# GDN and mLSTM layers on one core: order of the first products, and the first head's second gate in seven products

## The chip, the cores and the metric

The kernel runs on one core of a Trainium2 chip. The time is the device time of one execution in microseconds. The core's engines are TensorE (PE, matmuls), VectorE (DVE), ScalarE (ACT), GpSimd (POOL) and SyncE (SP, whose queue issues the transfers). TensorE's clock has two levels, 1.2 and 2.4 GHz; the profile gives the granted clock as a share of the full one.

## The reference

x has 1024 tokens of 1024 channels. Two residual layers follow each other, a gated DeltaNet (GDN) and an mLSTM, and then a final RMSNorm. Each has 8 heads, with 128 channels for queries and keys and 256 for values.

```python
def gdn_mixer(h, w_in, ...):                    # layer 0, h = rmsnorm(x)
    qkv, z, a, bt = split(h @ w_in)
    q, k, v = split(silu(causal_dwconv(qkv)))   # q and k are then l2-normed
    g, beta = -exp(a_log) * softplus(a + dt_bias), sigmoid(bt)
    o = gated_delta_chunked(q, k, v, g, beta)
    return (rmsnorm(o) * silu(z)) @ w_out

def mlstm_mixer(h, w_in, ...):                  # layer 1, h = rmsnorm(x + y0)
    qk, v, og, z, ig, fg = split(h @ w_in)
    q, k = split(silu(causal_dwconv(qk)))
    hc = mlstm_chunked(q, k * 128 ** -0.5, v, ig + i_bias, log_sigmoid(fg + f_bias))
    gate = sigmoid(og) * silu(z)                # the first gate and the second gate
    return (rmsnorm(hc) * gate) @ w_out
```

## The kernel before, in words

**Layout.** Everything is kept with channels on the 128 partitions. h is eight tiles of channels (k), each in two halves of 512 tokens. Every operand of a large product is split into a big part (`hi`, rounded, made by ScalarE) and a small part (`lo`, the rest, made by VectorE or GpSimd), and a product is the sum of three matmuls: hi x hi, hi x lo, lo x hi. For h these parts are `hh` and `hl` (lines 261 to 270, `prenorm`: eight products on VectorE, eight casts on ScalarE, eight subtractions; `VLO` names those that VectorE does).

**Projections.** A plain projection (`proj_half`, line 290) takes 128 columns of a weight and one half of the tokens: 8 tiles k of three matmuls with 512 columns each. A `Pair` (line 563) takes 256 columns and both halves together in seven products in place of eight: each product is four tiles of three matmuls, on blocks of h (A11, A12, A21, A22) and on sums of these blocks (S1, S2, S3 from `h_blocks`, line 469, S4 from `last_block`, line 484). It needs sums of weight blocks as well, which VectorE makes (`operands`), and additions on the way out.

**Order.** PE's instructions are issued in the order in which the program writes them. On the other engines a planner orders by readiness in its own simulation and by program order; `tc.issue_after` holds instructions behind a given one. Generators yield after each step (on PE mostly three matmuls), and tables say at which step of the projections a piece of other work is written: `FIRST` for the first mLSTM head, `KEYS`, `QUERIES`, `MERGE`, `TOKENS`, `SCAN`, `BLOCKS`, `LAST` for the GDN heads (first, second, others), `NORM0` for the norm of the second half of h.

**The GDN start.** `first_qk` runs, for each half of the tokens, k's projection and then q's. In the first half each tile of k is followed by two matmuls of the gate columns (`gate_columns`). The norm of the second half is written between steps: its sums (`n_cs`) and the reciprocal root at step 4, the broadcast (`n_rs`) and the parts of h at step 9. In the second half the gate columns run first, then k, then q.

**The first mLSTM head.** After its keys, queries and half of its values the loop at line 1559 runs 80 steps: 16 of values for the second half of the tokens (`mlstm_v`), then 64 of `first_gates`, which computes the output gate (`mog`) and the second gate (`mz`) by plain projections, two column tiles of two halves of eight steps each. In `FIRST` the letters stand for: `g` the gate rows (`head_gates`: a chain of small operations), `p` the decay masks and the scaled keys (`mlstm_prepare`, which first makes `mkd` and later `mg`), `b` one tile of `h_blocks`, `l` one tile of `last_block`, `r` the first weights of the next pair, `s` the first steps of the scan. After the loop the pairs of the other heads follow, while the scan of this head goes on.

## Time and profile before

| | |
|---|---|
| three timed runs | 1934.71, 1935.31, 1938.71 us; median 1935.31 |
| profiled execution | 1938.76 us, its span 1937.0 us |
| PE busy | 1876.3 us (97%), 9776 matmuls |
| VectorE, ScalarE, GpSimd busy | 1252.5, 1010.6, 697.9 us |
| mean granted clock | 0.994 |

A busy PE is not one at its peak: matmuls are pipelined, and their starts, not their lengths, give the pace. Times in the rows count from the start of the span. An idle stretch matters where it is PE's, since PE is busy nearly all the time.

### The profile page before, as it was taken

The numbers are of one execution on the slowest core, as the hardware profiler recorded it, in microseconds if no ns is written. First come the engines' busy times: TensorE is split into PE (matmuls) and PEld (weight loads), VectorE is DVE, ScalarE is ACT, GpSimd is POOL, SyncE is SP. The second block draws the span as 40 slices with busy tenths as digits, with TensorE's granted clock in tenths as the row PEclk, the third lists the DMA queues.
The fourth block names the chain that finished last, engine by engine and source line by source line (L and its number), as shares of the span: only waits on it lengthen the run. The fifth ranks groups of instructions, "written<-read, shape, count | busy, mean of one in ns | idle before, by whom it ended". The sixth has DMA issues, their size and how long they took to land.

```text
span 1937.0 us, 28865 instructions
## 1 busy us (share of the span) xinstructions
PE 1876.3 (97%) x9776; PEld 1548.2 (80%) x9776; DVE 1252.5 (65%) x2845; ACT 1010.6 (52%) x2332; POOL 697.9 (36%) x661
## 2 busy tenths in 40 slices
PE   5899999999999999999999999999999999999998
PEld 3687888887787778787878788888888888888886
DVE  6679686858585858647556866666666666673413
ACT  5555455555555565645445454555554545564423
POOL 4234334343434333100121334333333333345553
PEclk9999999999999999999999999999999999999999
DMA  4211122222222222646321221212122212245342
GB/s 143 79 60 44 55 72 82 56 81 63 69 67 73 71 62 76 205 135 217 116 77 57 79 74 60 76 56 80 63 76 69 74 62 73 76 138 172 137 138 73
DMA packets 138620, 171.24 MB, mean 88 GB/s; under 512 B 30860, under 2 KB 68584, under 8 KB 138472
## 3 DMA queue, kind: packets, MB, share of 16 engines
q1 hardware_dynamic: 137896, 168.87, 27.7%
q8 instruction: 77, 1.26, 0.3%
q14 instruction: 71, 0.58, 0.1%
q10 hardware_dynamic: 576, 0.52, 0.1%
HBM read 142.87 MB, written 26.48 MB: 87 GB/s over the span
## 4 chain that ended last, share of the span: by engine, by line
PE 81%; DVE 6%; ACT 5%; DMA 3%; issue 1%; POOL 1%; SPq 0%; DVEq 0%; ACTq 0%; POOLq 0%
PE lout L699 8%; PE gzp_ps L500 7%; PE gout L699 7%; PE mkq_ps L500 7%; PE mv_ps L500 7%; PE gkv_ps L500 7%; PE mz_ps L500 6%; PE mog_ps L500 6%; PE gqv_ps L500 6%; PE o L1066 1%; PE mo L1487 1%; PE y L1049 1%; PE mv_ps L1237 1%; PE ks L1044 1%; PE sn L1056 1%
## 5 line engine op out<-in xcount | busy, mean ns | idle before, releaser
L414 POOL TENSOR_TENSOR g_r<-g_r,mhalf 128x1 f32<-128x1 f32 x64 | 39.9, 623 | 209.3 <-DVE g_r L413 207.5
L284 DVE SCALAR_TENSOR_TENSOR gw_lo<-gw_raw,rest,gw_hi 128x256 fp32r<-128x256 f32 x128 | 64.4, 540 | 64.3 <-ACT gw_hi L283 64.3
L279 POOL TENSOR_TENSOR lw_lo<-lw_raw,lw_hi 128x512 fp32r<-128x512 f32 x56 | 72.7, 1301 | 72.6 <-ACT lw_hi L278 67.0
L279 POOL TENSOR_TENSOR mog_lo<-mog_raw,mog_hi 128x512 fp32r<-128x512 f32 x39 | 50.3, 1291 | 115.1 <-ACT mog_hi L278 115.1
L283 ACT ACTIVATE gw_hi<-gw_raw,rest 128x256 fp32r<-128x256 f32 x128 | 57.9, 501 | 62.5 <-PE gout L699 36.2
L699 PE MATMUL lout<-lgp_hh,lw_hi 128*128 128x512 f32 x224 | 88.4, 395 | 1.2 <-DVE mg L1357 1.2
L279 POOL TENSOR_TENSOR mz_lo<-mz_raw,mz_hi 128x512 fp32r<-128x512 f32 x39 | 53.1, 1363 | 99.7 <-ACT mz_hi L278 99.7
L699 PE MATMUL lout<-lgp_hh,lw_lo 128*128 128x512 f32 x224 | 87.3, 390 | 0.0
L699 PE MATMUL lout<-lgp_hl,lw_hi 128*128 128x512 f32 x224 | 87.2, 389 | 0.0
L279 POOL TENSOR_TENSOR mv_lo<-mv_raw,mv_hi 128x512 fp32r<-128x512 f32 x38 | 52.4, 1379 | 84.9 <-ACT mv_hi L278 55.2
L500 PE MATMUL gkv_ps<-hh,gkv_hi 128*128 128x512 f32 x176 | 78.2, 444 | 0.0
L278 ACT CAST lw_hi<-lw_raw 128x512 fp32r<-128x512 f32 x56 | 34.7, 620 | 79.1 <-PE lout L699 52.2
L279 POOL TENSOR_TENSOR gkv_lo<-gkv_raw,gkv_hi 128x512 fp32r<-128x512 f32 x40 | 52.2, 1304 | 63.2 <-ACT gkv_hi L278 58.4
L279 POOL TENSOR_TENSOR mkq_lo<-mkq_raw,mkq_hi 128x512 fp32r<-128x512 f32 x35 | 45.1, 1289 | 76.0 <-ACT mkq_hi L278 66.7
L279 POOL TENSOR_TENSOR gzp_lo<-gzp_raw,gzp_hi 128x512 fp32r<-128x512 f32 x38 | 50.4, 1325 | 56.7 <-ACT gzp_hi L278 46.0
L500 PE MATMUL gkv_ps<-hh,gkv_lo 128*128 128x512 f32 x176 | 69.3, 394 | 0.0
L500 PE MATMUL gkv_ps<-hl,gkv_hi 128*128 128x512 f32 x176 | 69.1, 393 | 0.0
L279 POOL TENSOR_TENSOR gqv_lo<-gqv_raw,gqv_hi 128x512 fp32r<-128x512 f32 x30 | 38.8, 1292 | 81.6 <-ACT gqv_hi L278 41.4
L699 PE MATMUL gout<-glp_hh,gw_hi 128*128 128x512 f32 x160 | 66.5, 415 | 0.0
L414 POOL TENSOR_TENSOR m_r<-m_r,mhalf 128x1 f32<-128x1 f32 x64 | 42.8, 669 | 64.1 <-DVE m_r L413 58.9
L699 PE MATMUL gout<-glp_hh,gw_lo 128*128 128x512 f32 x160 | 62.7, 392 | 0.0
L699 PE MATMUL gout<-glp_hl,gw_hi 128*128 128x512 f32 x160 | 62.4, 390 | 0.0
(773 smaller groups left out, 6657.9 us busy)
## 6 DMA issues: line engine op xcount, KB each, us to landing
gw_raw<-in_gdn_w_out_dram SPq DMA_DIRECT2D x64, 256.0 KB, 2.7
lw_raw<-in_mlstm_w_out_dram SPq DMA_DIRECT2D x56, 256.0 KB, 2.7
gzp_raw<-in_gdn_w_in_dram SPq DMA_DIRECT2D x32, 256.0 KB, 3.3
growb<-g_dram SPq DMA_DIRECT2D x32, 256.0 KB, 3.2
gg_dram<-gv_h SPq DMA_DIRECT2D x64, 128.0 KB, 1.8
gl<-gg_dram SPq DMA_DIRECT2D x32, 256.0 KB, 3.2
mog_raw<-in_mlstm_w_in_dram SPq DMA_DIRECT2D x32, 256.0 KB, 3.2
mz_raw<-in_mlstm_w_in_dram SPq DMA_DIRECT2D x32, 256.0 KB, 3.0
```

Source lines behind the costliest of these rows:

```text
L278: A.copy(hi, raw)
L279: (e or G).tensor_tensor(lo, raw, hi.bitcast(F32), ALU.subtract)
L283: A.activation(hi[:, k], raw[:, k], AF.Copy, scale=c)
L284: V.scalar_tensor_tensor(lo[:, k], raw[:, k], c, hi.bitcast(F32)[:, k], ALU.mult, ALU.subtract)
L414: G.tensor_tensor(r, r, mhalf[:, :1], ALU.pow)
L500: mm(ps, w_[:, k, :], h_, start=first and k == 0 and i == 0, stop=k == 3 and i == 2, skip_group_check=True)
L699: mm(pss[2 * j + i], a[:, e, i * P:(i + 1) * P], b, start=h == heads[0] and e == 0 and m == 0, stop=h == heads[-1] and e == ET - 1 and m == 2)
L1044: mm(ks[:, :DV], k[:, s_], S, start=True, stop=True)
L1049: mm(yp[:, :DV], st["tt"][half][:, cc, :], rr, start=True, stop=True)
L1056: mm(spn[:, :DV], st["kd"][half][:, cc, :], w, start=True, stop=True)
L1066: mm(op[:, :DV], st["at"][half][:, cc, :], w, start=S is None, stop=True)
L1237: mm(ps[c], h_[k][half][:, c * P:(c + 1) * P], w_[:, k % 2, :], start=k == 0 and i == 0, stop=k == KT - 1 and i == 2)
```

## The change

Three things change.

In the GDN start, k's projection of head 0 and the gate columns use the small part of tile n four tiles behind the big part (`LAG`, `behind_by`): steps 0 to 3 have big parts only, steps 4 to 6 use the small parts 0 to 2, and step 7 the small parts 3 to 7. The matmuls are the same. The norm of the second half moves to steps 8 and 10.

In the GDN plan, the steps of the head-0 queries, the second head's merge and scan, the last token step of the other heads, the first block of `h_blocks` and the four of `last_block` move.

In the mLSTM layer, the first head's second gate (z) becomes a `Pair`. The loop has 76 steps: 16 of values, 32 of the output gate, 28 of the pair. For this one pair (`late`) the second product is A12 in place of S2, and its weights are split in that order. `h_blocks` moves from steps 42, 46, 50, 54 to 16, 22, 27, 32 and is no longer held behind the gate rows; `last_block` from 72 to 78 to 41 to 47; the two `mg` steps from 54 and 60 to 51 and 56; the pair's weights are loaded at step 26, and two of its operands are split at steps 39 and 42 (`a`). The silu of z is written in place for every head.

```diff
@@ -32,9 +32,11 @@
 NB = P // BLK
 NG4 = P // (NB * NT)
 HT = 4
-NORM0 = (4, 9)
+NORM0 = (8, 10)
 NORM1 = ((-1, 4, 8), (-1, 9, 15))
 RAW = 3
+
+LAG = 4
 QB, AB = 4, 4
 WB, GB = 2, 2
 OUT0 = "k", "wraw"
@@ -44,8 +46,8 @@
 R8 = range(8)
 LOOK = 2
 VLO = (((1, 3, 6, 7), (1, 2, 3, 5, 7)), ((3, 6, 7), (1, 3, 5, 7)))
-FIRST = {0: "g", 13: "g", 18: "g", 23: "g", 28: "g", 33: "p", 37: "p", 42: "b", 46: "b", 50: "b", 54: "bp", 60: "pr", 68: "s",
-         72: "l", 74: "l", 76: "l", 78: "l"}
+FIRST = {0: "g", 13: "g", 16: "b", 18: "g", 22: "b", 23: "g", 26: "r", 27: "b", 28: "g", 32: "b", 33: "p", 36: "p", 39: "a", 41: "l",
+         42: "a", 43: "l", 45: "l", 47: "l", 51: "p", 56: "p", 67: "s"}
 UNITS = ({u: "ss" for u in range(14, 27, 2)},
          {0: "v", 1: "v", 2: "vt", 3: "vp", 4: "p", 6: "p", 8: "p", 11: "s",
           **{u: "ss" for u in (13, 15, 17, 19, 22, 24, 26)}, 28: "s"})
@@ -54,15 +56,15 @@
 
 
 KEYS = ((4, 9, 10, 17), (26, 29, 30, 33), (22, 25, 26, 29))
-QUERIES = ((19, 22, 25, 32), (68, 71, 76, 76), (80, 80, 84, 89))
+QUERIES = ((20, 22, 25, 32), (68, 71, 76, 76), (80, 80, 84, 89))
 SOLVE = (24, 41, 38)
-MERGE = (78, 96, 89)
-TOKENS = ((37, 37, 81, 85), (74, 77, 100, 106), (64, 74, 103, 106))
-SCAN = (95, 113, 102)
+MERGE = (78, 97, 89)
+TOKENS = ((37, 37, 81, 85), (74, 77, 100, 106), (64, 74, 103, 109))
+SCAN = (95, 110, 102)
 PACE = ((3, 3, 8), (4, 3, 10), (4, 3, 11))
-BLOCKS = (101, 115, 114, 126)
+BLOCKS = (106, 115, 114, 126)
 XLOADS = (24, 116)
-LAST = (156, 158, 157, 159)
+LAST = (158, 148, 156, 164)
 TH = HT * P
 
 
@@ -287,12 +289,21 @@
     def split_halves(w, c0, name, raws=None):
         return [split(t, f"{name}_{i}") for i, t in enumerate(raws or load_halves(w, c0, name))]
 
-    def proj_half(parts, name, half, sink):
+    def behind_by(k, lag):
+
+        return range(max(k - lag, 0), KT) if k == KT - 1 else range(k - lag, k - lag + 1) if k >= lag else ()
+
+    def proj_half(parts, name, half, sink, lag=0):
         ps = pwork(f"{name}_ps{half}", "p")
         for k in range(KT):
             hi, lo = parts[k // 4]
-            for i, (w_, h_) in enumerate(((hi, h_hi), (hi, h_lo), (lo, h_hi))):
-                mm(ps, w_[:, k % 4, :], h_[k][half], start=k == 0 and i == 0, stop=k == KT - 1 and i == 2)
+            mm(ps, hi[:, k % 4, :], h_hi[k][half], start=k == 0, stop=False)
+            if lag:
+                mm(ps, lo[:, k % 4, :], h_hi[k][half], start=False, stop=False)
+            for n in behind_by(k, lag):
+                mm(ps, parts[n // 4][0][:, n % 4, :], h_lo[n][half], start=False, stop=lag > 0 and n == KT - 1)
+            if not lag:
+                mm(ps, lo[:, k % 4, :], h_hi[k][half], start=False, stop=k == KT - 1)
             if k == KT - 1:
                 sink(half, ps)
             yield
@@ -349,7 +360,7 @@
                 for _ in gates:
                     pass
             for parts, nm, sink in ((kparts, "k", sinks[0]), (qparts, "q", sinks[1])):
-                for _ in proj_half(parts, f"{name}{nm}0", half, sink):
+                for _ in proj_half(parts, f"{name}{nm}0", half, sink, LAG if name == "g" and nm == "k" else 0):
                     if step < KT:
                         next(gates)
                     between(step)
@@ -565,6 +576,7 @@
 
 
         spare = False
+        late = False
 
         def __init__(self, w, ca, cb, name, sink, dst=lambda e, half: None, u2=None, engines=None,
                      in_psum=(True, True), bank="x"):
@@ -583,8 +595,11 @@
             yield part(1, b11, G)
             V.tensor_tensor(b12, b12, b22, ALU.subtract)
             V.tensor_tensor(b11, b11, b12, ALU.subtract)
-            yield part(6, b11, e6)
+            if not self.late:
+                yield part(6, b11, e6)
             yield part(2, b21, G)
+            if self.late:
+                yield part(6, b11, e6)
             V.tensor_tensor(b21, b21, b11, ALU.subtract)
             V.tensor_tensor(b11, b22, b11, ALU.subtract)
             yield part(5, b11, e5)
@@ -601,13 +616,15 @@
             yield from product(p1, "A11", operand())
             A.copy(u2, p1)
             yield
-            p6 = pwork(f"{name}_ps6", "b")
-            yield from product(p6, "S2", operand())
-            V.tensor_tensor(u2, u2, p6, ALU.add)
-            yield
-            yield from product(p1, "A12", operand(), False)
-            sink(0, 0, p1)
-            yield
+            for second in (self.late, not self.late):
+                if second:
+                    yield from product(p1, "A12", operand(), False)
+                    sink(0, 0, p1)
+                else:
+                    p6 = pwork(f"{name}_ps6", "b")
+                    yield from product(p6, "S2", operand())
+                    V.tensor_tensor(u2, u2, p6, ALU.add)
+                yield
             u4 = wp.tile([P, TH], F32, tag="wraw", bufs=WB, name=f"{name}_u4")
             p5 = pwork(f"{name}_ps5", "p")
             yield from product(p5, "S1", operand())
@@ -741,7 +758,7 @@
     accs = [squares_of(half * HT, HT, f"n0_{half}", "at", AB) for half in range(2)]
     prenorm(0, 0, rstd_of(sums_of(accs[0], "n0_0"), "n0_0"))
 
-    def gate_columns(raw, name, res):
+    def gate_columns(raw, name, res, lag=0):
 
         n = 2 * H
 
@@ -752,9 +769,9 @@
         for half in range(2):
             ps = pwork(f"{name}_ps{half}", "d")
             for k in range(KT):
-                for i, h_ in enumerate((h_hi, h_lo)):
-                    mm(ps[:2 * n, :], wg[:, k, :], h_[k][half], start=k == 0 and i == 0,
-                       stop=k == KT - 1 and i == 1)
+                mm(ps[:2 * n, :], wg[:, k, :], h_hi[k][half], start=k == 0, stop=False)
+                for m in behind_by(k, lag):
+                    mm(ps[:2 * n, :], wg[:, m, :], h_lo[m][half], start=False, stop=m == KT - 1)
                 if k == KT - 1:
                     row = hp.tile([2 * n, TH], F32, tag="acc", bufs=3, name=f"{name}_row{half}")
                     A.copy(row, ps[:2 * n, :])
@@ -775,7 +792,7 @@
     gt = sp.tile([P, 2 * H, NT], F32, tag="td", bufs=1, name="gt")
 
     def gdn_gates():
-        yield from gate_columns(wg0, "ggate", gt)
+        yield from gate_columns(wg0, "ggate", gt, LAG)
         V.tensor_tensor(hc(a_t), gt[:, :H, :], dtb.unsqueeze(2).to_broadcast([P, H, NT]), ALU.add)
         A.activation(hc(beta), gt[:, H:, :], AF.Exp, scale=-1.0)
         V.tensor_scalar(beta, beta, 1.0, None, ALU.add)
@@ -1349,12 +1366,9 @@
             A.activation(gate(half)[:, e, :], src, AF.Sigmoid)
 
         def z_sink(e, half, src):
-            sz = src
-            if h == 0:
-                sz = hp.tile([P, TH], F32, tag="acc", bufs=3, name=f"msz{h}_{e}_{half}")
-            A.activation(sz, src, AF.Silu)
+            A.activation(src, src, AF.Silu)
             g = gate(half)[:, e, :]
-            V.scalar_tensor_tensor(g, g, mnw[:, e:e + 1], sz, ALU.mult, ALU.mult)
+            V.scalar_tensor_tensor(g, g, mnw[:, e:e + 1], src, ALU.mult, ALU.mult)
 
         return o_sink, z_sink, lambda e, half: gate(half)[:, e, :]
 
@@ -1365,12 +1379,11 @@
 
     def first_gates(st):
 
-        o_sink, z_sink, _ = gate_sinks(0, st)
-        for nm, c0, sink in (("mog", 2 * QK + DI, o_sink), ("mz", 2 * QK + 2 * DI, z_sink)):
-            for e in range(ET):
-                parts = split_halves(w1, c0 + e * P, f"{nm}0_{e}")
-                for half in (1, 0):
-                    yield from proj_half(parts, f"{nm}0_{e}", half, lambda half, ps: sink(e, half, ps))
+        o_sink = gate_sinks(0, st)[0]
+        for e in range(ET):
+            parts = split_halves(w1, 2 * QK + DI + e * P, f"mog0_{e}")
+            for half in (1, 0):
+                yield from proj_half(parts, f"mog0_{e}", half, lambda half, ps: o_sink(e, half, ps))
 
     def parts_of(t, hi, lo, name, e=G):
 
@@ -1548,21 +1561,22 @@
         sts_m = [st] + [{"v": []} for _ in range(H - 1)]
         pairs = []
         for h in range(H):
-            if h:
-                pairs += gate_pairs(h, sts_m[h])
+            pairs += gate_pairs(h, sts_m[h])[0 if h else 1:]
             if h < H - 1:
                 pairs += [keys_pair(h + 1, sts_m[h + 1]), values_pair(h + 1, sts_m[h + 1])]
-        for pair in pairs[1::2]:
+        for pair in pairs[::2]:
             pair.spare = True
+        pairs[0].late = True
         sources.extend(sources_of(pairs))
         todo = iter(pairs)
-        for i, _ in enumerate(steps_of(mlstm_v(0, st, 1, vparts, VT[1]), first_gates(st))):
+        for i, _ in enumerate(steps_of(mlstm_v(0, st, 1, vparts, VT[1]), first_gates(st), next(todo).products())):
             for g in FIRST.get(i, ""):
                 if g == "b":
-                    with tc.issue_after(st["gates"].ins):
-                        do(hb)
+                    do(hb)
                 elif g == "r":
                     pairs[0].load()
+                elif g == "a":
+                    ahead(len(ready) + 1)
                 else:
                     do({"g": hg, "p": prep, "l": lb, "s": scan}[g])
         ahead(LOOK)
```

## Rows read from the trace of the kernel before

**Rows 1.** The page, sections 1 and 4: busy share of engines; chain by engine.

```profile
PE 1876.3 (97%) x9776; PEld 1548.2 (80%) x9776; DVE 1252.5 (65%) x2845; ACT 1010.6 (52%) x2332; POOL 697.9 (36%) x661
...
PE 81%; DVE 6%; ACT 5%; DMA 3%; issue 1%; POOL 1%; SPq 0%; DVEq 0%; ACTq 0%; POOLq 0%
```

**Rows 2.** PE's waits: waiter, line, released by; us in total, times, longest.

```profile
PE gk_ps L295 <- DVE hl L270: 4.0, 1, 4.0
...
PE mg L1414 <- DVE mkd_lo L1405: 2.5, 1, 2.5
...
PE ggate_ps L756 <- DVE hl L270: 1.9, 1, 1.9
...
PE kq L940 <- DVE nt L914: 1.0, 1, 1.0
```

**Rows 3.** PE's timeline, head: start, length, line, operation, [idle before, releaser].

```profile
21.52 0.80 PE L295 MATMUL gk_ps<-hh,gk_hi 128*128 128x512 f32 x1 [2.44 <-ACT hh L269]
...
29.35 0.79 PE L295 MATMUL gk_ps<-hl,gk_hi 128*128 128x512 f32 x1 [4.04 <-DVE hl L270]
...
36.59 0.95 PE L235 MATMUL n_cs<-ones,n_sq 128*128 128x1 f32 x8
...
40.96 0.39 PE L295 MATMUL gq_ps<-hh,gq_hi 128*128 128x512 f32 x1
...
42.36 1.02 PE L258 MATMUL n_rs<-n_diag,ones 128*128 128x512 f32 x2
...
55.15 0.50 PE L295 MATMUL gk_ps<-hh,gk_hi 128*128 128x512 f32 x1
```

**Rows 4.** Stretches: us; busy of PE, PEld, DVE, ACT, POOL; PE clock; DMA.

```profile
28.50:35.30 6.80, 5.95 (x14) 3.73 (x15) 3.80 (x6) 0.00 (x0) 0.24 (x1) 0.50 0.00 0
1026.00:1048.00 22.00, 22.00 (x146) 19.32 (x144) 6.80 (x25) 9.36 (x16) 1.56 (x2) 1.00 0.12 39
1048.00:1072.00 24.00, 21.52 (x98) 17.31 (x97) 22.62 (x39) 18.47 (x38) 6.60 (x4) 0.95 0.30 98
```

**Rows 5.** VectorE's timeline, head of the program.

```profile
27.75 2.75 DVE L270 TENSOR_TENSOR hl<-x,hh 128x512 fp32r<-128x512 f32 x3
...
31.02 0.68 DVE L270 TENSOR_TENSOR hl<-x,hh 128x512 fp32r<-128x512 f32 x1
...
38.87 0.69 DVE L251 TENSOR_TENSOR n_diag<-ident,n_rc 128x512 f32<-128x512 f32 x1 [1.12 <-POOL n_rc L249]
...
43.42 4.04 DVE L266 SCALAR_TENSOR_TENSOR x<-x,nwc,n_rs 128x512 f32<-128x512 f32 x6
```

**Rows 6.** ScalarE's timeline, head of the program.

```profile
23.15 3.52 ACT L269 CAST hh<-x 128x512 fp32r<-128x512 f32 x6
...
48.87 1.28 ACT L318 ACT_TABLE_LOAD   x1
```

**Rows 7.** PE's timeline, first mLSTM head.

```profile
1062.32 0.50 PE L295 MATMUL mz_ps<-hh,mz_hi 128*128 128x512 f32 x1
...
1069.92 2.08 PE L1414 MATMUL mg<-mqT,mkT 128*128 128x128 f32 x8 [2.46 <-DVE mkd_lo L1405]
...
1076.49 1.05 PE L1414 MATMUL mg<-mqT,mkT 128*128 128x128 f32 x8
...
1091.05 0.39 PE L500 MATMUL mkq_ps<-hh,mkq_hi 128*128 128x512 f32 x1
```

**Rows 8.** The chain that ended last, second gate: start, us, what.

```profile
1083.72 7.49 PE mz_ps L295 x33
```

**Rows 9.** VectorE's timeline, and tile S4hl: ns min/median/max, first and last start.

```profile
1066.01 1.79 DVE L458 TENSOR_TENSOR S3hl<-hs,S3hh 128x512 fp32r<-128x512 f32 x1
...
1069.53 0.59 DVE L1405 SCALAR_TENSOR_TENSOR mkd_lo<-mtp,wkey,mkd 128x128 fp32r<-128x128 f32 x2
...
L458 DVE TENSOR_TENSOR S4hl<-hc,S4hh x4: 673/686/693, 1082.5 to 1097.6; 128x512 fp32r<-128x512 f32 x4
```

**Rows 10.** GpSimd's timeline, same stretch.

```profile
1063.37 3.88 POOL L279 TENSOR_TENSOR mz_lo<-mz_raw,mz_hi 128x512 fp32r<-128x512 f32 x2 [10.25 <-ACT mz_hi L278]
```

## The prediction

> **What bounds the kernel now.** I read the page first. TensorE (PE) is busy for 97% of the span and holds 81% of the chain that ended last [rows 1]. A change can therefore pay in three ways only: fewer matmuls, fewer idle gaps on PE, or less time at the lower clock. The second view was the list of PE's waits [rows 2]. Besides the start of the program it is short, and four of its stalls stand where the change works: 4.0 us for a small part of h, 1.9 us for another in the gate columns, 1.0 us ahead of the first kq, and 2.5 us ahead of mg in the first mLSTM head. The third view was PE's timeline of the head of the program [rows 3] with the granted clock by stretch [rows 4]: after the 4.0 us stall PE ran 28.5 to 35.3 at 0.50 (1.2 of 2.4 GHz), where a 512-column matmul takes 0.43 us (14 in 5.95) instead of 0.23 [rows 8]. Then I read the engines that feed these places [rows 5, 6], and the same for the first mLSTM head [rows 7 to 10].
>
> **GDN: small parts four tiles behind.** No matmul is added or removed; the order alone changes. PE begins gk at 21.52 [rows 3]. The big parts hh come from ScalarE, six of them in 3.52 us from 23.15, the last at about 26.7 [rows 6]; three of the four small parts that VectorE makes come at 27.75 to 30.5 [rows 5]. In the old order the second k tile needs its small part, and PE stops from 25.3 to 29.35. In the new order steps 0 to 3 need only big parts. Walked through (three matmuls in steps 0 to 3, five in 4 to 6, thirteen in 7, 40 in all): steps 0 to 2 are paced by the low clock and the arrival of hh until about 25.4; from there a matmul takes 0.23 if the clock then rises as it did in the profiled run and does not fall. Step 3 ends at 26.1 and step 4 at 27.2. Step 5 waits for the first VectorE small part until about 28.7 (a third of the way through the group at 27.75) and ends at 29.4. Step 6 ends at 30.5 and step 7, held a little by the last small part near 31.7 [rows 5], at 33.5. The old end of the same work was 40.96 with the n_cs sums inside it (0.8), so 40.15. That is 6.6 us.
>
> Not all of it is kept, because the sums of the second half are now queued behind this work (step 8 instead of 4) and the norm at step 10 instead of 9. In the old run n_cs started at 36.59 and the diagonal was ready at 39.56 [rows 3, 5], 2.97 us later, with slack before n_rs at 42.36. New: n_cs starts at 34.2, the diagonal is ready at 37.2, and only six matmuls (1.4 us) stand between n_cs and n_rs: PE waits about 0.8 us, a new wait, with the rest of gq half 0 queued behind it. n_rs then starts at 37.2 to 38, 4.4 to 5.1 us earlier than before. From n_rs to gk half 1 the old run took 12.8 us (42.36 to 55.15), paced by eight products on VectorE from 43.42, the casts on ScalarE, the subtractions, and the gate columns behind them. Here a little more goes: a table load of 1.28 us for the first silu on ScalarE [rows 6] stood among the casts, and part of the convolution of gk among the products; both now come due before them. I take 1 us for that. So gk half 1 starts 5.5 us earlier. From below: if the norm of the second half is the whole limit and the queues shift against it, 2 us; from above, if nothing is lost, 7.5 us. The kq step (20 instead of 19) gives three more matmuls (0.7 us) of cover to a 1.0 us stall [rows 2]: 0.7 us, between 0 and 1. The other moved steps (merge, scan and tokens of later heads, the blocks, the last block) carry the same instructions at other places in PE's order. They add and remove no work on PE; I cost them at nothing, since VectorE's fillers are hidden behind 97% of matmul, with plus or minus 3 us as the bound: 3 us is about what one stall like mg's with its clock is worth (below). The scan of head 1 now begins one step after its last merge product, so a ScalarE copy has 0.7 us instead of 3.4 us to land; that is inside the 3.
>
> **mLSTM: the first head's second gate in seven products.** Old: four half projections of 24 matmuls, 96. New: seven products of 12, 84. In the chain 33 such matmuls took 7.49 us [rows 8], 0.227 each: 12 x 0.227 = 2.7 us less on PE. This is as good as certain.
>
> The old stage ran from 1062.32 to 1091.05 [rows 7], 28.7 us. Of that 96 x 0.227 = 21.8 is mz; 2.5 is the wait for mg; two groups of mg at full clock are 2.1 (the second one's 1.05 each); six scan matmuls of half the columns are some 0.7 (an estimate, half of 0.227 each); the rest, 1.7 us, is the clock: the first mg group took 2.08 instead of 1.05 and the matmuls behind it ran slow, right after the wait. So that wait is worth 2.5 + 1.7 = 4.2 us.
>
> Does it go? mg waits for a PSUM buffer that mkd_lo reads; the last of its readers ends at 1069.9 [rows 9]. These run in turns with ScalarE's mkd copies and were late because VectorE was full: 22.62 us of 24 in 1048 to 1072, after only 6.80 of 22 in 1026 to 1048 [rows 4]. What filled it were the block sums, held back behind the gates. The change moves the four h_blocks steps to 16, 22, 27, 32 and drops that hold. Each is six 128x512 operations on VectorE of 0.68 us (the S4 row's median [rows 9]), 4.1 us, 16.3 us for four, and the idle 15.2 us of 1026 to 1048 is where they can now go. Against it: mg stands at step 51 instead of 54, 2 us earlier; the last block (four times four operations, 10.9 us) is now due at steps 41 to 47; and the pair brings eleven VectorE operations that the plain projection did not have (four differences of weights, two small parts, five additions), 7.5 us, four more ScalarE casts and copies, and one more GpSimd subtraction. The pair's four weight loads are as large as the four that they replace; they are issued at step 26, past nothing that waits. The loads of mkq's weights now follow at step 39, ahead of the decay rows for mg on SyncE's queue, and the first of them waits for a buffer that the pair frees; if SyncE holds to that order, the rows come late for the second chunk of the scan, which has some 15 steps to spare. The silu of z in place costs what it did: the same four activations and products. I cost the loads and the silu at nothing, and their bound is the stage's. Work on VectorE from 1026 to PE's need of S4 near 1079 is then about 6.8 + 16.3 + 10.9 + 7.5 + 7 (the attention's own masks, mkd_lo and products) = 48.5 us in 53. It fits, barely, so I don't expect PE to pass without any wait: I put 2 us back. Net: 2.7 + 4.2 - 2 = 4.9 us; from below 0 (waits of 7 us), from above 7.
>
> At one place a page speaks against this. The row: with GpSimd in two mz_lo subtractions (3.88 us [rows 10]) a VectorE subtraction took 1.79 us instead of 0.68 [rows 9]. The Trainium skill, "SBUF — State Buffer", section "Who interferes with whom", says that a VectorE instruction with two SBUF inputs and a GpSimd instruction that reads SBUF exclude each other on a shared port. The trace agrees. By that rule each of the pair's five GpSimd subtractions would cost VectorE up to 1.1 us, 5.5 us in all, and the sum of the stage would be nearer its lower end.
>
> **Sum.** 5.5 + 0.7 + 4.9 = 11.1 us. Against the profiled execution: 1938.8 - 11.1 = 1927.7. The three timed runs have their median 3.4 us below that execution (1935.3, one of the three as high as it); the same difference gives 1935.3 - 11.1 = 1924.2.
>
> **The rivals.** *VectorE takes it back in the mLSTM stage.* Lockstep chain, S sums and S4 on one full engine; mg at step 51 waits as long as before, and the clock falls again. For it: 22.62 of 24 us, the exclusion above, mg earlier by three steps. Against it: 15 idle us ahead of it. The stage nets 0: 1935.3 - 5.5 - 0.7 = 1929.1.
>
> *The second half's norm takes back the head.* PE gets to n_rs early and waits there, and again in the gate columns, since that chain hangs on VectorE and ScalarE. For it: the 1.9 us stall there now. Against it: sums and diagonal are earlier too. The head nets 1: 1935.3 - 1 - 0.7 - 4.9 = 1928.7.
>
> *Slower: S4 comes too late.* In the old run the four small parts of S4 ended between 1083 and 1098.3 [rows 9], and nobody wanted them before the sixth product of mkq, 20 steps of 0.68 us after 1091.05 [rows 7]. Now the sixth product of mz wants the last near 1080.5 (1062.3 + 23 steps of 0.68 + mg and scan). If VectorE's fillers don't move forward, PE waits 17.8 us and loses about 2 at the low clock, as after mg: 1935.3 + 19.8 - 2.7 - 4.2 - 6.2 = 1942.0. It decides the sign once the last part is later than about 1091. The single buffer hc, in which each block waits for the one before, speaks for it; the free stretch before speaks against it.
>
> *Both gains lost.* First and second rival together leave about 1 us: 1934.5, no change that can be told.
>
> **How the numbers follow.** Forecast 0.50, first rival 0.21, second 0.13, slower 0.08, no change 0.08. The predicted time is the forecast's, 1924.2, its own range 1919 to 1929. For 8 in 10 the range takes in the first two rivals and the 3 us of the moved steps on either side: 1917 to 1932. About 0.2%, 3.9 us, is what a measurement of this kernel can tell from no change: faster by more 0.83, within it 0.08, slower by more 0.09 (the rival and a little of the moved steps).
>
> **What would show it.** Right: no PE gap at 25 to 29, the clock high from about 25 on; gk half 1 starting near 49.6 instead of 55.15; VectorE nearly full in 1026 to 1048 of the old scale; mz to mkq in some 24 us instead of 28.7, with no drop of the clock there; PE's waits 8 to 10 us shorter in total and 12 matmuls fewer. Wrong: a wait of PE on S2, S3 or S4 parts in mz of more than 3 us; a stall before n_rs over 2 us; new stalls between 100 and 250 us, where steps were moved.

## The result, and the profile after

The changed kernel takes 1924.79 us (median of four runs, 1924.03 to 1925.56) where the kernel before took 1935.07 in the same set (four runs, 1934.71 to 1938.71). That is 10.3 us faster by the medians. The ratio of the means is 0.9943, with a 95% interval of [0.9931, 0.9955], which is 11 us (9 to 13). The forecast was 1924.2. The profiled execution of the changed kernel took 1924.86 us, its span 1923.1. That is 13.9 us less than the profiled execution of before, because the latter lies 3.4 us above the median of its three timed runs. A comparison of these two traces has some 3 us in it that the timed runs don't have.

Busy time of the engines on the page of the kernel after, beside [rows 1]: twelve matmuls are gone, and the other engines have 3 to 6 us more work. PE's idle time (span less busy time) falls from 60.7 to 51.1 us, 9.6 us; the forecast had 8 to 10.

```profile
PE 1872.0 (97%) x9764; PEld 1545.2 (80%) x9764; DVE 1256.2 (65%) x2856; ACT 1016.1 (53%) x2336; POOL 701.4 (36%) x662
```

PE's waits after (us in total, times, longest), to be read beside [rows 2]:

```profile
PE n_rs L260 <- DVE n_diag L253: 4.2, 2, 3.5
PE tpk L886 <- DVE kd L910: 3.3, 6, 0.8
PE kk L928 <- DVE nt L931: 2.8, 1, 2.8
...
PE ggate_ps L774 <- DVE hl L272: 2.0, 2, 1.0
PE kq L957 <- DVE nt L931: 1.8, 1, 1.8
...
PE gk_ps L304 <- DVE hl L272: 0.3, 1, 0.3
```

The two large stalls at which the change aims are gone or small: 4.0 us for hl is now 0.3 (1.5 in `a_again` below, the same kernel once more), and 2.5 us for mkd_lo stands nowhere. The wait ahead of kq has grown from 1.0 to 1.8. And there is a line that [rows 2] did not show, because the prediction passed over it: tpk waiting for kd. In the kernel before it was the largest wait after the start of the program:

```profile
PE tpk L869 <- DVE kd L893: 7.3, 5, 1.6
```

PE's timeline of the head after (start, length, line, operation, [idle before, releaser]), beside [rows 3]:

```profile
21.46 0.80 PE L300 MATMUL gk_ps<-hh,gk_hi 128*128 128x512 f32 x1 [2.44 <-ACT hh L271]
...
29.34 0.50 PE L304 MATMUL gk_ps<-hl,gk_hi 128*128 128x512 f32 x1 [0.27 <-DVE hl L272]
...
34.30 0.39 PE L300 MATMUL gq_ps<-hh,gq_hi 128*128 128x512 f32 x1
34.98 0.95 PE L237 MATMUL n_cs<-ones,n_sq 128*128 128x1 f32 x8
...
38.09 1.10 PE L260 MATMUL n_rs<-n_diag,ones 128*128 128x512 f32 x2 [0.65 <-DVE n_diag L253]
...
42.46 1.09 PE L772 MATMUL ggate_ps<-hh,ggate_w 128*32 128x512 f32 x4
...
45.98 0.42 PE L774 MATMUL ggate_ps<-hl,ggate_w 128*32 128x512 f32 x1 [0.97 <-DVE hl L272]
...
47.66 0.42 PE L774 MATMUL ggate_ps<-hl,ggate_w 128*32 128x512 f32 x1 [1.03 <-DVE hl L272]
...
51.83 0.80 PE L300 MATMUL gk_ps<-hh,gk_hi 128*128 128x512 f32 x1
```

gq starts 6.7 us earlier than before (34.30 against 40.96; 0.8 of it only because the sums n_cs now stand behind it), n_rs 4.3 us (38.09 against 42.36), k of the second half 3.3 us (51.83 against 55.15), and that one runs slowly. The granted clock by stretch (us; busy of PE, PEld, DVE, ACT, POOL; PE clock; DMA) shows why, beside [rows 4]:

```profile
28.50:35.30 6.80, 6.54 (x31) 4.29 (x29) 5.24 (x11) 1.42 (x3) 0.23 (x1) 1.00 0.00 0
48.16:54.99 6.83, 6.73 (x22) 4.09 (x22) 4.54 (x14) 2.46 (x3) 0.00 (x0) 0.50 0.07 20
55.00:61.80 6.80, 6.80 (x31) 5.63 (x30) 5.43 (x17) 2.25 (x6) 2.62 (x2) 1.00 0.12 40
```

The slow stretch 28.5 to 35.3 has become a fast one, 31 matmuls instead of 14. A new slow stretch, 48.16 to 54.99 at 0.50 (1.2 of 2.4 GHz), stands behind the gate columns, where PE idled 0.5, 1.0 and 1.0 us within 4 us. It holds 22 matmuls, the 6.8 us behind it 31. What it costs can be read from `u_mlstm` below, which has the same GDN program and the same three waits and stays at 1.00 from 46 to 56: there the first matmul of cum starts 43.3 us after the first of gk, here 45.1 (66.51 less 21.46). So this drop costs 1.7 us up to that point.

PE's timeline of the first mLSTM head after, beside [rows 7]:

```profile
1053.84 0.50 PE L511 MATMUL mz_ps<-hh,mz_hi 128*128 128x512 f32 x1 [0.63 <-ACT mg L1366]
...
1056.71 1.05 PE L1427 MATMUL mg<-mqT,mkT 128*128 128x128 f32 x8
...
1058.09 0.50 PE L511 MATMUL mz_ps<-hh,mz_hi 128*128 128x512 f32 x1 [0.33 <-ACT mz_u L617]
...
1061.63 1.05 PE L1427 MATMUL mg<-mqT,mkT 128*128 128x128 f32 x8
...
1071.67 0.47 PE L511 MATMUL mz_ps<-S4hh,mz_hi 128*128 128x512 f32 x1 [0.78 <-DVE mz_u L631]
...
1077.23 0.39 PE L511 MATMUL mkq_ps<-hh,mkq_hi 128*128 128x512 f32 x1
```

Both mg groups take 1.05 us and neither is waited for. From the first mz to mkq it is 23.4 us instead of 28.7. In place of the mg wait stand three small ones, 1.7 us in all, the first of them (0.63) just ahead of the first mz and so outside the 23.4. VectorE in the same stage, its stretches and its timeline, beside [rows 4, 9]:

```profile
1017.50:1039.50 22.00, 21.53 (x139) 18.66 (x138) 16.79 (x45) 11.78 (x22) 2.29 (x3) 1.00 0.24 80
...
1053.80:1077.20 23.40, 22.26 (x106) 18.52 (x107) 20.58 (x31) 12.13 (x24) 11.96 (x8) 1.00 0.21 68
```

```profile
1054.94 0.34 DVE L1418 SCALAR_TENSOR_TENSOR mkd_lo<-mtp,wkey,mkd 128x128 fp32r<-128x128 f32 x1
...
1069.47 0.68 DVE L469 TENSOR_TENSOR S4hl<-hc,S4hh 128x512 fp32r<-128x512 f32 x1
```

The stretch ahead of the stage now has 16.79 us of VectorE work where 6.80 stood. The last mkd_lo ahead of the first mg ends at 1055.3, 1.4 us before mg starts; before, mg started as the one it waited for ended (1069.9). S4's last part starts at 1069.47 instead of 1097.6, 28 us earlier, of which 8.5 are the lead that PE has at the first mz.

### The profile page after: what moved, and what is told of

Read it like the earlier page. It is cut to its first block, busy times and chain, and to the rows that moved or that the text cites. A ratio compares the mean times of both kernels' runs of the same rounds, so it can differ in the third digit from the quotient of the medians.

```text
span 1923.1 us, 28886 instructions
## 1 busy us (share of the span) xinstructions
PE 1872.0 (97%) x9764; PEld 1545.2 (80%) x9764; DVE 1256.2 (65%) x2856; ACT 1016.1 (53%) x2336; POOL 701.4 (36%) x662
## 3 DMA queue, kind: packets, MB, share of 16 engines
q8 instruction: 77, 1.26, 0.3%
## 5 line engine op out<-in xcount | busy, mean ns | idle before, releaser
L281 POOL TENSOR_TENSOR mkq_lo<-mkq_raw,mkq_hi 128x512 fp32r<-128x512 f32 x35 | 45.1, 1289 | 75.2 <-ACT mkq_hi L280 61.8
```

Of the source, the lines that this page charges most:

```text
L281: (e or G).tensor_tensor(lo, raw, hi.bitcast(F32), ALU.subtract)
```

## The experiments

Two accounts stand against each other. By the prediction's sum the lag gives most, the mLSTM stage the rest and the moved GDN steps nothing. By what the two traces suggest, most of the lag's gain is given back, and one of the moved steps carries the GDN side. Ratios are to the kernel before, run in the same set; interval 95%. The kernel after was timed in two sets, 0.9943 [0.9931, 0.9955] and, as `a_again`, 0.9958 [0.9944, 0.9972].

### Four runs that undo one part each

`u_lag`: the lag undone.

```diff
-NORM0 = (8, 10)
+NORM0 = (4, 9)
-LAG = 4
+LAG = 0
```

> The changed kernel with the GDN start put back: small parts of h in their old place in k's projection and the gate columns, second half's norm at steps 4 and 9. Theory A (the gain is three separate shares: GDN start about 4.2 us by PE's lead at 100 us, moved token step about 4.5 us by the shorter waits before tpk, mLSTM stage about 4.0 us; together 10.3 in the timed medians, so each a little smaller there): 3 to 4.5 us slower than the changed kernel, 1928 to 1929.3, with the 4 us gap at 25 to 29 us back. Theory B (what PE wins at the start is given back at the gate columns of the second half and at kq, where new waits and a drop of the clock stand): at most 1 us slower, 1925 to 1926.

`u_tok`: the last token step of heads 2 to 7 back.

```diff
-TOKENS = ((37, 37, 81, 85), (74, 77, 100, 106), (64, 74, 103, 109))
+TOKENS = ((37, 37, 81, 85), (74, 77, 100, 106), (64, 74, 103, 106))
```

> The changed kernel with one number put back: the last token step of heads 2 to 7 at 106 instead of 109. Theory A (that step took the ScalarE copy out of the way of the squares that release tpk's buffer): PE's waits before tpk go from 3.3 back to some 7.3 us in all, and the time is 3 to 5 us up, 1928 to 1930. Theory C (these waits got shorter because the planner's order shifted with everything else): the waits stay near 0.56 us a head, and the time is within 1 us, 1924 to 1926.

`u_plan`: the other moved GDN steps back.

```diff
-QUERIES = ((20, ...   MERGE = (78, 97, 89)   SCAN = (95, 110, 102)
-BLOCKS = (106, 115, 114, 126)   LAST = (158, 148, 156, 164)
+QUERIES = ((19, ...   MERGE = (78, 96, 89)   SCAN = (95, 113, 102)
+BLOCKS = (101, 115, 114, 126)   LAST = (156, 158, 157, 159)
```

> The changed kernel with the other moved GDN steps put back (queries of head 0, merge, scan and first block sums of head 1, the last block), the token step kept. Theory A: nothing that can be told, within 1.5 us, 1923.5 to 1926.5, since in the profile PE's lead hardly moves between 95 and 300 us. Theory C (the order of fillers on VectorE that these steps set is what shortened the later waits): 3 to 5 us slower, 1928 to 1930.

`u_mlstm`: the kernel before with the GDN side of the kernel after.

> The changed GDN layer with the mLSTM layer of before (second gate of the first head by plain projections, block sums at their old steps behind the gate rows). Theory A: the stage's share is 2.7 us for the twelve matmuls and some 1.3 to 2 us for the wait of mg with its clock less the new waits: 3.5 to 4.7 us slower than the changed kernel, 1928.3 to 1929.5, the wait before mg back at about 2.5 us. Theory D (the mg wait was an accident of the one profiled execution, and the stage pays for the matmuls alone): 2.4 to 3 us slower, about 1927.5.

Measured: `u_lag` 0.9957 [0.9944, 0.9970], `u_tok` 0.9965 [0.9953, 0.9977], `u_plan` 0.9951 [0.9936, 0.9965], `u_mlstm` 0.9972 [0.9959, 0.9985]. Against the mean of the two sets of the kernel after (0.99505) the undone parts cost about 1.3, 2.8, 0.1 and 4.2 us (difference of ratios times 1935), each with some 3 us of uncertainty. Against the first set alone the lag is 2.7 us, against `a_again` -0.2. So by these times the mLSTM stage is clear of noise, and the lag is worth between nothing and some 4 us, under the forecast's 5.5; how it ranks beside the token step they can't tell, and the traces below decide that. In `u_lag` the 4.0 us stall at 29.12 is back in full, and yet little time is lost: neither of its theories is shown by the time alone. The other three came out as their theory A had it, `u_tok` a little under its 3 us.

`u_tok` brings the waits for kd back, and nothing else of that size:

```profile
PE tpk L886 <- DVE kd L910: 7.0, 6, 1.4
```

In `u_mlstm` the wait ahead of mg is back (start, length, [idle before, releaser], then the granted clock of the stretch behind it):

```profile
1061.72 1.16 PE L1425 MATMUL mg<-mqT,mkT 128*128 128x128 f32 x8 [2.43 <-DVE mkd_lo L1416]
```

```profile
1062.93:1066.34 3.41, 3.41 (x9) 2.67 (x8) 2.71 (x5) 2.48 (x4) 1.55 (x1) 0.50 0.53 190
```

### One part alone

`t_alone`: the kernel before with the token step alone.

```diff
-TOKENS = ((37, 37, 81, 85), (74, 77, 100, 106), (64, 74, 103, 106))
+TOKENS = ((37, 37, 81, 85), (74, 77, 100, 106), (64, 74, 103, 109))
```

> The kernel before with one number changed: the last token step of heads 2 to 7 is written at step 109 in place of 106. Theory T (the moved step is a term of its own, mis-sized at nothing in the prediction): in the kernel before PE waits five times for kd ahead of tpk, 1.37 to 1.65 us each, 7.3 us in all; in the kernel after the same waits are 0.21 to 0.81. Alone it should take these waits to about 3.3 us in all and the time down by about 4 us (2.5 to 5), the pitch of the middle heads from 91.8 to 91.1 us. Theory C (the waits fell because of something else in the new plan, or what is won is given back to a later wait of the same head): the waits stay at 1.37 or the pitch does, and the time is within 1.5 us of before.

Measured: 0.9983 [0.9975, 0.9992], 3.2 us faster (1.5 to 4.8). The waits:

```profile
PE tpk L869 <- DVE kd L893: 2.9, 5, 0.7
```

4.4 us of waiting are gone, and the distance from one head's wait to the next, read from their starts, fell from 91.8 us (346.23, 438.10, 529.81) to 90.9 (343.27, 434.19, 525.13). Theory T holds: one number in a table is worth about a third of the whole change.

ScalarE's timeline shows what the number moved, in the kernel before and then in `t_alone` (ahead of the first of the five waits; a table load, and the last of the four squares of the keys):

```profile
341.24 1.28 ACT L901 ACT_TABLE_LOAD   x1
...
345.09 0.27 ACT L872 ACTIVATE sqrk<-tpk 128x128 bf16<-128x128 f32 x1
```

```profile
338.09 1.28 ACT L901 ACT_TABLE_LOAD   x1
...
342.12 0.28 ACT L872 ACTIVATE sqrk<-tpk 128x128 bf16<-128x128 f32 x1
```

By the rows kd starts when the last square has ended (its releaser is sqrk), and tpk waits for kd. PE's kk just before starts at 343.11 and at 340.96. So the last square comes 1.98 us after kk in the kernel before and 1.16 in `t_alone`. In the kernel before ScalarE takes one square ahead of the table load and puts the cast of gqv_hi and the scan's w among the other three; in `t_alone` the load comes 1.0 us earlier against kk, and w stands behind the last square. All five waits of the kernel before and all five of `t_alone` go with this order (last square 1.98 to 2.25 us and 1.16 to 1.26 after kk).

`m_alone`: the kernel after with the GDN side of before (`LAG = 0`, all tables of the GDN heads as before).

> The kernel after with the whole GDN side of before: only the mLSTM change is left. Theory M (the stage's gain is its own: 12 matmuls fewer, the mg wait and the clock drop behind it gone, small new waits): 3 to 5.5 us faster than before, with mz to mkq in about 23.5 us in place of 28.7, no wait of PE for mkd_lo. Theory D (part of it hangs on the GDN change, by another start of the stage): the wait ahead of mg or a new one of over 1.5 us stands there, and less than 2 us is left.

Measured: 0.9970 [0.9960, 0.9981], 5.8 us faster (3.7 to 7.7). There is no wait for mkd_lo, and mz to mkq is 23.4 us (1060.79 to 1084.15). Theory M holds; by the medians it is 5.0 us.

`m_alone` also shows where the lag's gain goes, since it has the GDN start of before and the program of the kernel after elsewhere. The same matmuls in both, first `m_alone`, then the kernel after (PE's timeline):

```profile
40.41 0.39 PE L300 MATMUL gq_ps<-hh,gq_hi 128*128 128x512 f32 x1
...
46.75 0.40 PE L772 MATMUL ggate_ps<-hh,ggate_w 128*32 128x512 f32 x1
...
49.53 0.41 PE L774 MATMUL ggate_ps<-hl,ggate_w 128*32 128x512 f32 x1 [1.92 <-DVE hl L272]
...
54.60 0.50 PE L300 MATMUL gk_ps<-hh,gk_hi 128*128 128x512 f32 x1
...
68.78 0.39 PE L813 MATMUL cum<-a_t,ones 128*128 128x64 f32 x2
...
78.35 1.05 PE L928 MATMUL kk<-gkT 128*128 128x128 f32 x8
...
89.98 1.05 PE L957 MATMUL kq<-gqT,gkT 128*128 128x128 f32 x8
...
299.05 0.39 PE L511 MATMUL gzp_ps<-S3hh,gzp_hi 128*128 128x512 f32 x1
```

```profile
66.90 0.39 PE L813 MATMUL cum<-a_t,ones 128*128 128x64 f32 x2
...
73.82 1.05 PE L928 MATMUL kk<-gkT 128*128 128x128 f32 x8
...
87.42 1.16 PE L957 MATMUL kq<-gqT,gkT 128*128 128x128 f32 x8 [1.83 <-DVE nt L931]
...
298.05 0.39 PE L511 MATMUL gzp_ps<-S3hh,gzp_hi 128*128 128x512 f32 x1
```

The lead of the kernel after is 6.1 us at gq (40.41 against 34.30), 4.3 at the first gate column of the second half (46.75 against 42.46), 2.8 at gk of that half (54.60 against 51.83), 1.9 at cum, 4.5 at kk (where `m_alone` has its own slow stretch, 72.09 to 75.51, and a wait of 2.18 for gr_ps in place of 1.13), 2.6 at kq, and 1.0 at 299 us. So five of the six microseconds are given back:

- 1.8 us before the gate columns: the sums, now behind gq (0.8), and the new wait at n_rs.
- 1.5 us in the gate columns. PE's waits there add up to 2.5 us in both traces (1.92, 0.29 and 0.30 in `m_alone`; 0.51, 0.97 and 1.03), so the work after the waits gives the difference: in the kernel after the last gate columns and the transposes run at 0.50.
- 0.9 more up to cum, where the first matmuls of gk still run at 0.50.
- The rest later. At kq PE meets nt, which VectorE ends only 2.0 us earlier (at 87.36 against 89.31), so the lead of 4.5 falls to 2.6. Between kq and 299 us the lead is 1.8 at kk of the second head (155.17 against 153.35, both behind a wait of 2.85) and 0.2 at 157.5, because a slow stretch follows in the kernel after (153.97 to 157.39) and none in `m_alone`; waits of 0.77 and 0.39 us at 160 to 163, which only `m_alone` has, give some back.

So the last step hangs on a drop of the clock that not every execution has. Over more traces: counted from the first gk, the same matmul at 299 us starts after 276.1 to 277.3 us in six traces with the lag (the kernel after, `a_again`, `l_late`, `u_tok`, `u_plan`, `u_mlstm`) and after 277.8 to 278.6 in four without it (`m_alone`, `t_alone`, `b_sums`, `u_lag`). By the means the lag leads by some 1.4 us there, whatever the other GDN steps are.

### The block sums moved, and nothing else

`b_sums`: the kernel before with the four tiles of `h_blocks` at the steps of the kernel after, without the hold behind the gate rows.

```diff
-FIRST = {0: "g", 13: "g", 18: "g", 23: "g", 28: "g", 33: "p", 37: "p", 42: "b", 46: "b", 50: "b", 54: "bp", ...
+FIRST = {0: "g", 13: "g", 16: "b", 18: "g", 22: "b", 23: "g", 27: "b", 28: "g", 32: "b", 33: "p", 37: "p", 54: "p", ...
-                    with tc.issue_after(st["gates"].ins):
-                        do(hb)
+                    do(hb)
```

> The kernel before with one thing alone: the four h_blocks steps of the first mLSTM head at 16, 22, 27, 32 and not held behind the gate rows; second gate by plain projections as before. Theory A (mg waits because VectorE is full of block sums at that place): the wait of 2.4 us before mg falls under 0.5, no stretch at 0.50 follows it, and the time falls by 2.5 to 4.5 us against before. Theory E (the lockstep of mkd and mkd_lo between ScalarE and VectorE sets it, whatever else is queued): the wait stays above 1.5 us and the time falls by less than 1 us.

Measured: 0.9997 [0.9988, 1.0006], no change that can be told. Neither theory came out as written. The wait ahead of mg is gone and the clock doesn't fall there: mz to mkq takes 24.3 us (1061.27 to 1085.60) instead of 28.7, so this wait with its clock is worth 4.4. But two new waits stand ahead of the stage (PE's timeline of `b_sums`):

```profile
1025.22 0.36 PE L1237 MATMUL mv_ps<-mv,hh 128*128 128x256 f32 x1 [0.93 <-DVE mkT L317]
...
1035.62 0.30 PE L1295 MATMUL rp<-ident,lf 128*64 128x128 f32 x1 [1.46 <-DVE lf L1289]
```

Against the kernel before, the lead shrinks by 2.8 us between 983 and 1036 and grows by 4.6 from there to mkq, net 1.8 us: VectorE's timeline has the early block sums among the steps of mkT and of the chain of the gate rows that lf ends. So the late steps or the hold, which this run drops together, did have a use. In `m_alone` the same block sums stand at the same steps, and the wait for lf is not there: VectorE makes the six like steps of that chain (ls_td) in one go at 1023.02, where `b_sums` has them between block sums, up to 1033.4. Which of the other edits of FIRST does this I did not separate. The comparison with `m_alone` tells what the pair itself brings from mz to mkq: 23.4 us instead of 24.3. One of its three waits lies ahead of the first mz, and counted from the last matmul of mog it is 24.4 instead of 24.6. So of the 2.7 us of the 12 matmuls 0.2 is left in this stage; the rest goes to the waits and to PE's restarts behind them.

### Is S4 close to being late?

`l_late`: the kernel after with the four tiles of `last_block` 17 steps later.

```diff
-41: "l", 42: "a", 43: "l", 45: "l", 47: "l", 51: "p", 56: "p", 67: "s"}
+42: "a", 51: "p", 56: "p", 58: "l", 60: "l", 62: "l", 64: "l", 67: "s"}
```

> The kernel after with the four parts of S4 written at steps 58, 60, 62, 64 in place of 41, 43, 45, 47; the same instructions. It tests the prediction's rival on the slower side (S4 too late), by its own point: in the kernel after VectorE starts the last of the four small parts at 1069.5 and PE asks for the first S4 operand at 1070.9. Theory L (VectorE's order follows the place in the program, so the parts come some 8 to 11 us later): PE waits 4 to 9 us in the second gate for an S4 part and has the lower clock for a few us behind it; with 1 to 2 us lost to the clock, 5 to 10 us slower than the kernel after, so at or above the kernel before. Theory P (the planner pulls them forward, since VectorE has idle time ahead of them): the parts end within 3 us of where they did and the time is within 2 us of the kernel after.

Measured: 0.9939 [0.9926, 0.9951], the time of the kernel after. VectorE makes the parts where it made them (timeline of `l_late`, first and last of four; in the kernel after 1051.38 and 1069.47):

```profile
1051.02 0.69 DVE L469 TENSOR_TENSOR S4hl<-hc,S4hh 128x512 fp32r<-128x512 f32 x1 [0.17 <-ACT S4hh L468]
...
1069.11 0.68 DVE L469 TENSOR_TENSOR S4hl<-hc,S4hh 128x512 fp32r<-128x512 f32 x1
```

Theory P holds: for these fillers, at these two places, the table does not set the order on VectorE, the planner does. Since the parts did not move, the run says nothing on what a late S4 would cost. The slower rival, by its own point (the last part later than 1091), was far off; the price of it was not tried.

### The same kernel again

`a_again`: the kernel after, unchanged.

> The changed kernel as it is, beside the others of this call, so that differences of 2 to 5 us are read on one chip against one set of runs of the kernel before. All theories: 9.5 to 11.5 us faster than before. In its profile the clock falls at the gate columns (44 to 50 us) and at kk (153 us) may or may not show again: theory A says that the kernel loses about 1.7 us wherever a PE gap happens to be followed by a stretch at 0.50.

Measured: 0.9958 [0.9944, 0.9972], median 1929.5 beside 1936.2 of before: 8.1 us faster (5.4 to 10.8), under the 9.5 to 11.5 that were expected. Its trace has the slow stretches of the kernel after and one more, in the last GDN head:

```profile
49.62:56.44 6.82, 6.64 (x21) 4.44 (x21) 4.32 (x15) 2.89 (x5) 0.00 (x0) 0.50 0.07 20
155.43:158.84 3.41, 3.41 (x10) 2.69 (x9) 3.41 (x6) 0.72 (x2) 2.28 (x2) 0.50 0.59 169
773.24:776.65 3.41, 3.41 (x10) 2.64 (x9) 2.62 (x5) 2.41 (x6) 1.64 (x1) 0.50 0.29 89
```

So what a stall costs at the clock differs from one execution of a kernel to the next.

### Three attempts at a better version

`v1`: steps of the early GDN heads written later, so that PE does not meet them early.

```diff
-KEYS = ((4, 9, 10, 17), (26, 29, 30, 33), ...      QUERIES = ((20, 22, 25, 32), ...
+KEYS = ((4, 9, 10, 17), (26, 29, 30, 37), ...      QUERIES = ((20, 25, 28, 33), ...
-at_steps((2,), gdn_decay())
+at_steps((2, 4), gdn_decay())       # and a yield ahead of gr_ps
```

> The changed kernel, with cover put ahead of its three largest remaining PE gaps in the GDN layer: the second kk of head 1 at step 37 instead of 33, the first kq of head 0 at 25 instead of 22 (the third query step at 28, the last at 33), and the transpose of the decay rows two steps behind the sums instead of right behind them. Theory A (PE's gaps are lost time, and each costs its length and, where the clock falls after it, about 1.7 us more): gaps of 2.85, 1.8 and 1.1 us go, and one or two stretches at 0.50: 5 to 8 us faster than the changed kernel. Theory F (each gap only shows how late VectorE's chain of the head is, and the cover moves the wait to the next step of that chain): the gaps reappear at the solve, merge or scan of the same head, and the time is within 2 us of the changed kernel.

`v2`: `v1` with the first four steps of k in the second half (big parts only) ahead of the gate columns. The cut leaves out the key and decay steps of head 0, which move as said below.

```diff
+                if half and name == "g" and nm == "k":
+                    for _ in range(LAG):
+                        next(gen)
+                        between(step)
+                        step += 1
+                    run(gates)
```

> As v1, and in the second half of the GDN start four steps of k's projection (big parts only, eight matmuls) run ahead of the gate columns; the decay steps at 4 and 6 and the key steps of head 0 at 6, 10, 11, 18 to leave the gate rows their time. Theory A: the gaps of 0.5, 1.0 and 1.0 us in the gate columns go and the clock does not fall there; 2 to 5 us faster than v1. Theory F: the chain from the last small part over the gate rows to the decay sums sets the time, so PE waits at the decay sums instead; within 1 us of v1.

Measured: `v1` 0.9945 [0.9932, 0.9958], `v2` 0.9939 [0.9926, 0.9952]; the kernel after in the same set 0.9958. In `v1` the waits ahead of kk, kq and gr_ps are gone and others of 1.4, 3.1 and 3.6 us stand at 70, 102 and 160 us: these stalls, which engines off PE set, were moved, not removed, much as theory F had it. In `v2` the gate columns have one wait of 1.04 us instead of three, and the clock stays at 1.00 from 44 to 57; two other slow stretches (67.2 and 156.0) are left. That the columns are the reason isn't shown: in `u_mlstm` the clock stays up behind the three waits as well.

`v3`: `v2` with the later block sums and S4 of the GDN plan written later.

```diff
-BLOCKS = (106, 115, 114, 126)   LAST = (158, 148, 156, 164)
+BLOCKS = (106, 126, 130, 136)   LAST = (158, 160, 162, 164)
```

> The fastest variant so far (the kernel after with the keys of the second head, the squares of the first queries and the decay rows written later, and four steps of k in the second half ahead of the gate columns), now with the last three steps of the block sums at 126, 130, 136 in place of 115, 114, 126 and those of S4 at 158, 160, 162, 164. In that variant PE waits 3.5 us for a state S at 157 us while VectorE makes block sums between 144 and 160, and the lower clock holds for 6.8 us from there. Theory B (the sums push the scan on VectorE): the wait at 157 falls under 1 us and so does the drop of the clock; 3 to 6 us faster than that variant's 0.9939 of before, so about 0.991 to 0.993. Theory R (the chain of the scan itself, with its row sums, table load and convolution, is what is late, and the sums only fill holes): the wait stays over 2 us and the time is within 1.5 us of that variant.

Measured: 0.9931 [0.9917, 0.9944], median 1923.67, the fastest of all, beside 0.9939 of `l_late` in the same set, which is the kernel after in all that its trace shows. The wait that it was to remove is still there:

```profile
PE ks L1069 <- DVE S L1084: 3.5, 1, 3.5
```

Its theory B fell in its first number (wait under 1 us), and theory R is not shown either: between 145 and 158 us VectorE makes the same five operations of the sums in `v2` and in `v3`, each 0.5 us later as ks itself is, so the edit did not move there what it was to move. The three versions lie 0.0008 to 0.0019 under the kernel after of their set, inside the intervals. That they are better at all can't be told.

## Why the prediction was right, and where it was not

The total was right, 1924.2 against 1924.8, and that was luck in part: the mechanism of the mLSTM stage was right, the GDN side was not, and two errors of 3 to 4 us there cancelled.

*GDN start, forecast 5.5 us (2 to 7.5), wrong in size.* The walk up to n_rs came out nearly as told. The gap of 4.0 us went; gq starts at 34.30, where step 7 was to end at 33.5; the sums start at 34.98 (forecast 34.2), n_rs at 38.1 with a wait of 0.65 (37.2 to 38, and 0.8). Only the pace rose later than said: a matmul every 0.43 us until 27.4, not until 25.4. From n_rs to gk half 1 the run took 13.74 us instead of 12.79, so the 1 us put on it is right too. The step that failed is the next sentence, "So gk half 1 starts 5.5 us earlier". It takes the 1 us from the 6.6 us at gq, while n_rs, on which that stretch hangs, was only 4.4 to 5.1 us earlier: the prediction's own numbers give 3.4 to 4.1, and 3.3 was measured. Then the sum counts this lead as time saved, and that failed as well: 1.0 us is left at 299 us against `m_alone`, some 1.4 over ten traces, and about 1.3 in time by `u_lag`, with 3 of uncertainty. The drop of the clock behind the gate columns (1.7 us) had no step in the prediction. The second rival ("the head nets 1") was the better account of this term; the condition given against it ("sums and diagonal are earlier too") was true and did not decide.

*The kq step, forecast 0.7 us, wrong.* The number that was moved (19 to 20) is not kq's own step, which stands at 22 in both tables, but that of the squares before it, so there was no more cover. The stall of 1.0 us was not there to be won either: in `b_sums`, `t_alone` and `m_alone`, with the GDN order of before, PE doesn't wait at the first kq at all, so it belonged to one execution. With the lag PE comes earlier than nt does, which VectorE makes, and the wait is 1.8 to 2.0 in five traces. In `u_plan`, with the number back, there is no wait, but counted from the first gk, kq stands at 65.8 us there and at 66.0 in the kernel after.

*The other moved steps, forecast nothing (3 either way), the mis-sized term.* The token step is worth 3.2 us alone (1.5 to 4.8), about 2.8 when undone. I reasoned from VectorE's fillers being hidden and did not look up what waited on that step, though the list of waits had it as its largest line after the start; the order that it changed is ScalarE's. The other five moves together are worth 0.1, nothing that can be told.

*mLSTM, forecast 4.9 us (0 to 7), right.* `m_alone` has 5.8 (3.7 to 7.7), the undone part 4.2. Nearly all of it is the wait for mg with its clock; the pair, 2.7 less 2 in the forecast, nets 0.2 in the stage. The wait and its clock were put at 4.2 and measured 4.4 in `b_sums`; the forecast of 2 for new waits stands beside 1.7 in the kernel after; mz to mkq was to take some 24 us and took 23.4. VectorE in the stretch ahead was to be "nearly full" and is at 16.79 of 22, so there was more room than I counted, and the first rival's full engine did not come about. What I had not seen is that the early sums cost 2.8 us ahead of the stage when they are moved alone.

On the port that VectorE and GpSimd share: in the stage after, beside GpSimd's subtractions (four small parts of the pair, two of mat, one of mkq) three VectorE operations on 512 columns took 1.03, 1.66 and 1.85 us instead of 0.68 to 0.73, about 2.4 us in all, and none stood ahead of a wait of PE of over 0.8. Four of GpSimd's seven took 1.64 to 2.22 us instead of 1.3, so both engines lost. By the rule of the Trainium skill, "SBUF — State Buffer", section "Who interferes with whom", the prediction estimated up to 5.5 us. The trace agrees with the rule in kind, with half of that size on VectorE, and the stage's time does not show it.

Added up, the parts measured singly (3.2 for the tokens, 5.8 for mLSTM, 1.3 for the lag, 0.1 for the rest) are 10.4 us beside 10.3 for the whole. With 2 to 3 us of uncertainty in each, that is closer than it could be relied on; it says that no large part is missing. Of the signs named, the clear ones of being wrong did not come: no wait for S2, S3 or S4 parts, 0.65 us before n_rs, and the largest stall between 100 and 250 us, 2.85 at kk, stood there before (2.84). The rival "Both gains lost" has a slip in its sum: the first two rivals together leave 1 + 0.7, so 1933.6 and not 1934.5.

What stays open: the lag's worth in time to better than some 3 us, why ScalarE's planned order in the GDN heads turns on the one token step, and what keeps lf on time in the mLSTM head.

## What to carry to other kernels

When a table of steps changes, look up for each number what waits on that step before calling it hidden: a wait of 1.4 us that returns in every head was worth more than a single stall of 4 us. Subtract along the path: what stands behind a wait can lead by no more than what it waits for, and the lead at an earlier matmul says nothing on it. A gain at the start of a chain is given back as far as the next engine that sets the pace is not moved with it, so follow the lead of the same matmul through the trace until it stays constant, and count only that. Work that is taken from a full stretch of an engine to an idle one must be checked against the chain that lived in the idle one.

## What the runs showed of the hardware

The same wait costs the clock in one execution and not in the next. A wait of 2.85 us ahead of kk was followed by 3.4 us at 0.50 in the kernel after (153.97 to 157.39), and a wait of 2.90 there in `u_tok`, whose GDN steps up to that point are the same, by none. In `m_alone` none follows the wait of 2.85 either:

```profile
155.00:160.00 5.00, 4.11 (x21) 3.26 (x21) 5.00 (x11) 1.99 (x5) 2.29 (x2) 1.00 0.46 118
```

And three waits of 0.5 to 1.0 us close together, in gate columns where PE was at work between them, stood ahead of a slow stretch of 6.8 us in both traces of the kernel after, of 3.4 us in `u_plan` (from 48.76) and in `u_tok` (from 47.21, as the third wait ended), and of none in `u_mlstm`; the GDN start is the same program in all five. One wait of 1.04 us at the same place (`v2`) stood ahead of none. A wait of 1.45 us ahead of a kq in the last GDN head stood before the stretch at 773.24 in `a_again`; in the kernel after that wait is 0.73, and none follows.
